# Scores of two heads on the two row halves of the array, probabilities normalised on GpSimd, and the evictions of their transposes on two engines

## The chip, the cores and the metric

The kernel runs on one core of a Trainium2 chip. The metric is the device time of one execution in microseconds (us). Beside the totals stands a profile, which is one further execution with the hardware profiler on. PE is TensorE's matmul, PEld its load of stationary operands, DVE is VectorE, ACT is ScalarE, POOL is GpSimd, and SP is the engine that issues the DMAs.

## The reference

The reference is a small network on 256 tokens of width 1024, all in fp32: a block with sparse attention (called NSA here), experts and an embedding gate; a second such block with shared keys (MOBA); and a third block with two feed-forward layers around a mixer, whose second half is a dilated attention. Three places in it are dense softmax attention on 256 keys, 64 columns a head:

```
# NSA, selected keys (and the same on window keys), 16 heads, 4 key heads
s_s = einsum('bgrqd,bgqnld->bgrqnl', qc, k_g) - slopes * dist_s
p_s = masked_softmax(s_s, dist_s >= 0)
o_s = einsum('bgrqnl,bgqnld->bgrqd', p_s, v_g)
o = gc[0] * o_c + gc[1] * o_s + gc[2] * o_w
# MOBA, 16 heads, 4 key heads
s_own = einsum('bgrqd,bgld->bgrql', qc, ko) - slopes * dist_o    # causal
pr = softmax(sc)
# mixer, 8 heads: softmax of q k with slopes, a mask and a multiplicity of each key
```

The keys are normed per head (`rms_norm(to_heads(k), k_gain)`) in NSA and MOBA and taken as they are in the mixer.

## The kernel before

**Dense products.** Every weight comes in units of 1 MB on the SP queue (`unit`, L274) into a ring of nine buffers (pool `raw`). ACT makes a unit's high part (L291), DVE what it leaves (L292), and PE multiplies three times for one product (`mm3`, L304 to L306): 48 matmuls of up to 512 columns for a column chunk of 1024 rows and 256 tokens. PE's dense products are the bulk of the program.

**What sets the order.** The program is written as one sequence, and a scheduler orders each engine's instructions ahead of time, by what each one needs and by priorities (`ahead_by`); on the chip every engine then takes its own list strictly in turn. A buffer of a pool is handed out to its users in the order in which the program asks for them; `raw` serves weight units and also `kb`, the keys of the attention.

**Keys.** In NSA, between the units of the second and the third column chunk, `keys` (L541) takes two buffers of `raw`, one for each branch (selected keys, window keys); MOBA and the mixer take one each, also between two weights. Each holds, for four key pairs, the keys of two heads on the diagonal: head 0's 64 rows beside zeros, head 1's 64 rows beside zeros in the other columns. GpSimd writes the zeros (L544), which is the buffer's first write and needs nothing but the buffer. Later `k_T` (L528) norms the keys (square L493, sum L494 and L495, reciprocal root L314 to L323, multiply L535), PE transposes them (L347), and `put_k` (L548) copies each 64-row half out of PSUM, one half on ACT (L556), one on DVE (L558). In NSA the compressed keys are made at the same time (L641 to L685): hidden products, a GELU on ACT and DVE, second products, a norm and one transpose.

**Softmax.** `softmax_T` (L561) is called for each pair of heads: 16 times in NSA (8 pairs, 2 branches), 8 in MOBA, 4 in the mixer, 28 in all. A call makes two score matmuls on all 128 rows (L565: 128 queries by 2 heads by 128 keys; L567: the other 128 queries by 2 heads by 256 keys); four fused bias, scale and maximum steps on DVE (L574); four exponentials on ACT (L579); sums and reciprocals on DVE; four multiplications of the probabilities by their weight, the first on ACT (L592), three on DVE (L594); six PE transposes (L598 to L600) into two PSUM tiles, each copied to SBUF by ACT (L601, 128x384). `attend` (L604) multiplies them with the values: four matmuls on 64 output rows each (L608, L610). Buffers: two of `p` and two of `pT`, four PSUM tiles `a` for scores and four `b` for the rest. Between the calls stand column sums for a later layer (`fill`) and, in NSA and MOBA, the second half of the queries.

The names that follow: `w` in the rows of L347 is the tile with the normed keys, `b` and `a` are PSUM tiles, `hi` and `lo` the two parts of a weight, `e` the activations.

## Time and profile before

| | |
|---|---|
| three runs | 1141.98, 1141.98, 1138.62 us |
| median | 1141.98 us |
| span of the profiled execution | 1135.9 us |
| lies around the span (median less span) | 6.1 us |
| NSA, key chain and window chunk | 42 to 59 us of the span |
| NSA, softmax of 8 pairs | 84 to 170 us |
| MOBA, key chain and query product | 361 to 385 us |
| MOBA, softmax of 8 pairs | 387 to 425 us |
| mixer, softmax of 4 pairs | 882 to 904 us |

The profiled execution's own total is not among the numbers; its span, 1135.9 us, is the time from the first to the last instruction on the core, and the 6.1 us are what the median has beyond it. A change of the span is taken as a change of the total. The stages are told from each other by the lines that run in them. A matmul's record ends later than its last column goes in, so two matmuls that follow each other overlap in their records, and the distance of their starts is their cost to PE.

### The profile page before, as it was taken

How to read it: one execution, taken by the hardware profiler on the slowest of the kernel's cores; microseconds unless marked ns; L12 is line 12 of the kernel's file. 1: busy time of each engine (PE TensorE's matmuls, PEld its weight loads, DVE VectorE, ACT ScalarE, POOL GpSimd, SP SyncE). 2: the span in 40 equal slices, each digit the busy share in tenths (PEclk: the TensorE clock that was granted, in tenths of full speed). 3: DMA queues.
4: the chain of work that ended last, by engine and by line, in shares of the span. 5: the costliest groups of instructions: out<-in, count | busy, mean ns of one | idle time of the engine just before them, and what ended most of it. 6: DMA issues, size and time to landing. Idle time of an engine off the chain costs nothing.

```text
span 1135.9 us, 18442 instructions
## 1 busy us (share of the span) xinstructions
PE 1070.6 (94%) x7133; PEld 833.2 (73%) x7133; DVE 701.9 (62%) x1672; ACT 516.2 (45%) x995; POOL 74.3 (7%) x61
## 2 busy tenths in 40 slices
PE   7999999999989999998987999999989979999995
PEld 6885548666457667665545999899879759999994
DVE  6786784644378966543467656565684775554555
ACT  5446584222267674221254444433544634444443
POOL 3000000210010002100003000000210030000001
PEclk9999999899999999999999999999989989999998
DMA  9746767599975485798886456745675344554401
GB/s 375 296 185 262 277 225 304 196 372 396 416 273 170 180 336 198 286 389 323 314 350 242 168 186 213 284 173 186 224 301 175 123 185 149 174 187 159 146 22 38
DMA packets 46508, 268.57 MB, mean 236 GB/s; under 512 B 5328, under 2 KB 7120, under 8 KB 20432
## 3 DMA queue, kind: packets, MB, share of 16 engines
q1 hardware_dynamic: 46416, 267.34, 62.9%
q8 instruction: 58, 0.95, 0.3%
q14 instruction: 34, 0.28, 0.1%
HBM read 266.27 MB, written 1.05 MB: 235 GB/s over the span
## 4 chain that ended last, share of the span: by engine, by line
PE 46%; DVE 5%; ACT 1%; issue 0%; ACTq 0%; DVEq 0%
PE b L305 8%; PE b L304 8%; PE b L306 8%; PE a L304 5%; PE a L306 5%; PE a L305 5%; PE a L1054 1%; DVE nq L319 1%; DVE h L1483 1%; PE a L1094 1%; DVE rstd L323 1%; PE a L1107 1%; PE b L1460 1%; DVE w L1482 1%; PE b L1033 0%
## 5 line engine op out<-in xcount | busy, mean ns | idle before, releaser
L292 DVE TENSOR_TENSOR lo<-raw,hi 128x1024 fp32r<-128x1024 f32 (+2 forms) x220 | 256.1, 1167 | 197.7 <-ACT hi L291 195.5
L291 ACT ACTIVATE hi<-raw 128x1024 fp32r<-128x1024 f32 (+2 forms) x234 | 234.3, 1008 | 262.3 <-PE b L305 144.6
L304 PE MATMUL b<-e,hi 128*128 128x256 f32 x768 | 219.7, 286 | 2.9 <-ACT e L426 2.9
L305 PE MATMUL b<-e,hi 128*128 128x256 f32 x768 | 219.3, 285 | 0.1
L306 PE MATMUL b<-e,lo 128*128 128x256 f32 x768 | 218.9, 285 | 0.0
L304 PE MATMUL a<-hi,e 128*128 128x512 f32 (+2 forms) x512 | 199.9, 391 | 2.4 <-ACT e L364 1.8
L305 PE MATMUL a<-lo,e 128*128 128x512 f32 (+2 forms) x512 | 198.0, 387 | 0.0
L306 PE MATMUL a<-hi,e 128*128 128x512 f32 (+2 forms) x512 | 197.2, 387 | 0.5 <-DVE e L365 0.5
L304 PEld LDWEIGHTS b<-e,hi 128*128 128x128 f32 x768 | 149.2, 194 | 4.7 <-ACT e L426 3.6
L305 PEld LDWEIGHTS b<-e,hi 128*128 128x128 f32 x768 | 149.1, 194 | 1.0 <-DVE e L427 0.7
L306 PEld LDWEIGHTS b<-e,lo 128*128 128x128 f32 x768 | 149.1, 194 | 0.0
L304 PEld LDWEIGHTS a<-hi,e 128*128 128x128 f32 x512 | 96.8, 189 | 23.1 <-ACT e L364 2.9
L306 PEld LDWEIGHTS a<-hi,e 128*128 128x128 f32 x512 | 96.1, 188 | 20.7 <-DVE e L365 2.1
L305 PEld LDWEIGHTS a<-lo,e 128*128 128x128 f32 x512 | 96.9, 189 | 18.9 <-DVE lo L292 0.9
L1054 PE MATMUL a<-raw,e 128*32 128x256 f32 x832 | 73.5, 383 | 1.1 <-DVEq L1291 0.8
L579 ACT ACTIVATE p<-p,m 128x128 f32<-128x128 f32 (+1 forms) x96 | 42.6, 447 | 8.9 <-DVE m L574 6.6
L484 DVE TENSOR_TENSOR h<-h,a 128x512 f32<-128x512 f32 x48 | 32.0, 684 | 22.0 <-PE a L1107 14.7
L1054 PEld LDWEIGHTS a<-raw,e 128*32 128x32 f32 x832 | 31.4, 109 | 18.8 <-issue 2.1
L292 POOL TENSOR_TENSOR lo<-raw,hi 128x1024 fp32r<-128x1024 f32 (+1 forms) x14 | 31.4, 2267 | 205.1 <-ACT hi L291 205.0
L1097 ACT ACTIVATE w<-a,sv 128x512 fp32r<-128x512 f32 x32 | 21.6, 687 | 48.0 <-PE a L1094 47.6
L1094 PE MATMUL a<-wd,hT 128*32 128x512 f32 x256 | 43.3, 607 | 0.0
L1107 PE MATMUL a<-w,GT 128*128 128x512 f32 x128 | 36.3, 416 | 6.2 <-ACT w L1097 5.1
(322 smaller groups left out, 1424.3 us busy)
## 6 DMA issues: line engine op xcount, KB each, us to landing
raw<-in_ffn SPq DMA_DIRECT2D x62, 1024.0 KB, 4.8
raw<-in_moe_gu SPq DMA_DIRECT2D x52, 1024.0 KB, 8.4
raw<-in_w_ada SPq DMA_DIRECT2D x36, 1024.0 KB, 5.0
wd<-in_moe_dn SPq DMA_DIRECT2D x64, 512.0 KB, 7.0
raw<-in_w_gate SPq DMA_DIRECT2D x8, 1024.0 KB, 11.1
raw<-in_w_m_in SPq DMA_DIRECT2D x8, 1024.0 KB, 5.5
raw<-in_w_a_in SPq DMA_DIRECT2D x7, 1024.0 KB, 11.1
e<-in_moe_gu SPq DMA_DIRECT2D x6, 1024.0 KB, 9.5
```

What stands on the lines that cost most here:

```text
L291: nc.scalar.activation(hi[:, sl], raw[:, at], AF.Copy)
L292: eng.tensor_tensor(lo[:, sl], raw[:, at], hi[:, sl], op=OP.subtract)
L304: mm(out, l[0], r[0], start=start, stop=False, **kw)
L305: mm(out, l[0], r[1], start=False, stop=False, **kw)
L306: mm(out, l[1], r[0], start=False, stop=stop, **kw)
L319: nc.vector.scalar_tensor_tensor(q, y, h, y, op0=OP.mult, op1=OP.mult)
L484: self.nc.vector.tensor_tensor(self.h[:, t, sl], self.h[:, t, sl], ps, op=OP.add)
L579: nc.scalar.activation(p, p, AF.Exp, bias=m[:, i:i + 1], scale=-1.0, accum_out=den[:, i:i + 1])
L1054: nc.tensor.matmul(pgs[pp][32 * x:32 * x + 32], xg[:, k, o:o + 32], wg[kk][:, x], start=(k == 0), stop=(k == KT - 1))
L1094: nc.tensor.matmul(py[32 * x:32 * x + 32], hT[:, 32 * x:32 * x + 32], wd[2 * n + x // 2][:, x % 2], start=True, stop=True)
L1097: nc.scalar.activation(yh[:, sl], py, AF.Identity, scale=cw)
L1107: nc.tensor.matmul(ps, GT[:, t * P:(t + 1) * P], y[:, n * 512:(n + 1) * 512], start=(b == 0), stop=(b == len(back) - 1))
```

## The change

The keys of all branches are one buffer of `raw` (NSA takes one buffer where it took two), four pairs by 256 keys for each branch, without zeros; no memset is left, and the first write of the buffer is now the copy of the first transposed keys. That copy takes all 128 rows at once (128x512) and alternates between ACT and DVE. A call's scores are four matmuls, two for each head, with that head's 64 rows of queries and keys as operands; a head has a PSUM tile of its own. The number of columns of a call is the same: 2 x 128 + 2 x 256. The four multiplications of the probabilities go to GpSimd. Of the two copies of the transposed probabilities the second goes to DVE. Everything else is text (docstrings).

```diff
-    sw='svvv',
+    sw='gggg',
...
-    def keys(self):
-        kb = self.raw.tile([P, 4, 2, T], F32, tag="raw", name="kb")
-        for hf in range(2):
-            self.nc.gpsimd.memset(kb[64 * hf:64 * hf + 64, :, 1 - hf], 0.0)
-        return kb
+    def keys(self, n):
+        kb = self.raw.tile([P, n, 4, T], F32, tag="raw", name="kb")
+        self.KB = [kb[:, i] for i in range(n)]
...
     def put_k(self, idx, ps, gain):
-        for hf, eng in ((0, "s"), (1, "v")):
-            sl = slice(64 * hf, 64 * hf + 64)
-            dst = self.KB[idx // 4][sl, idx % 4:idx % 4 + 2, hf, :]
...
+        dst = self.KB[idx // 4][:, idx % 4:idx % 4 + 2]
+        if gain is None:
+            self.copy(dst, ps)
+        else:
+            self.copy(dst, ps, gain)
...
-            s0 = self.psa([P, 2, P])
-            nc.tensor.matmul(s0, QT[:, j, 0:P], kb[:, :, 0:P], start=True, stop=True)
-            s1 = self.psa([P, 2, T])
-            nc.tensor.matmul(s1, QT[:, j, P:T], kb, start=True, stop=True)
+            s = [self.psa([P, 3 * P]) for _ in range(2)]
+            for t in range(2):
+                for hh in range(2):
+                    sl = slice(64 * hh, 64 * hh + 64)
+                    nc.tensor.matmul(s[hh][:, t * P:t * P + (t + 1) * P], QT[sl, j, t * P:(t + 1) * P],
+                                     kb[sl, 0:(t + 1) * P], start=True, stop=True)
...
-            for i, (p, s, a, b) in enumerate(blocks):
-                if K["sw"][i] == "s":
-                    nc.scalar.activation(p, p, AF.Copy, scale=w[:, i:i + 1])
-                else:
-                    self.engine(K["sw"][i]).tensor_scalar(p, p, w[:, i:i + 1], None, op0=OP.mult)
+            for i, (o, x, a) in enumerate(blocks):
+                self.engine(K["sw"][i]).tensor_scalar(o, o, w[:, i:i + 1], None, op0=OP.mult)
...
-                nc.scalar.activation(pT[:, hh], ps, AF.Copy)
+                if hh:
+                    nc.vector.tensor_copy(pT[:, hh], ps)
+                else:
+                    nc.scalar.activation(pT[:, hh], ps, AF.Copy)
...
-        self.KB = [self.keys() for _ in range(2)]
+        self.keys(2)
...
-        self.KB = [self.keys()]
+        self.keys(1)
```

The change also moves instructions. The lines of the changed kernel are, behind `softmax_T`, four lower than before (L641 is L637, L347 stays). Numbers ahead of a row are its place in the engine's list. First PE in NSA, from the hidden products of the compressed keys on. Before:

```order
98 L641 MATMUL b<-raw,e 64x256 x32
99 L304 MATMUL a<-hi,e 128x304
100 L305 MATMUL a<-lo,e 128x304
101 L306 MATMUL a<-hi,e 128x304
...
115 L651 MATMUL b<-consts,x_398 128x128 x2
116 L305 MATMUL a<-lo,e 128x304
117 L306 MATMUL a<-hi,e 128x304
118 L304 MATMUL a<-hi,e 128x304
119 L665 MATMUL b<-small,w_407 128x64
120 L305 MATMUL a<-lo,e 128x304
```

And now:

```order
98 L637 MATMUL b<-raw,e 64x256 x32
99 L647 MATMUL b<-consts,x_398 128x128 x2
100 L661 MATMUL b<-small,w_407 128x64
101 L665 MATMUL b<-small,w_408 128x64
102 L661 MATMUL b<-small,w_407 128x64
103 L665 MATMUL b<-small,w_408 128x64 x7
104 L678 MATMUL b<-consts,kd 128x128
105 L347 MATMUL b<-consts,w_479 128x128 x8
106 L304 MATMUL a<-hi,e 128x304 x2
107 L305 MATMUL a<-lo,e 128x304
```

The products of the third chunk (128x304) stood directly behind the hidden products, with the small matmuls of the compressed keys between them one at a time; now all of these, and the eight transposes of the first branch's keys, stand ahead of the first product.

ACT at the same place. Before:

```order
14 L291 ACTIVATE hi<-raw 128x608 x4
15 L644 ACTIVATE x_398<-b 128x256
16 L647 ACTIVATE x_398<-x_398 128x256
17 L291 ACTIVATE hi<-raw 128x512
18 L657 ACTIVATE w_407<-b 128x4x16
```

And now:

```order
14 L640 ACTIVATE x_398<-b 128x256
15 L643 ACTIVATE x_398<-x_398 128x256
16 L653 ACTIVATE w_407<-b 128x4x16 x2
17 L670 ACTIVATE w_434,kcs<-b 128x64
18 L493 ACTIVATE w_458<-w_241 128x256
19 L493 ACTIVATE w_461<-w_241 128x256
20 L667 ACTIVATE vc<-b 128x256
21 L261 ACTIVATE kb<-b,small 128x512
22 L291 ACTIVATE hi<-raw 128x608 x4
```

The four splits of that chunk (128x608) stood ahead of the whole chain of the compressed keys; now they stand behind it and behind the first copy into `kb`.

PE in MOBA, around the transposes of the keys (L347), with the last products of keys and values above in the new list and products of the queries in all other rows. Before:

```order
1023 L306 MATMUL a<-hi,e 128x512
1024 L347 MATMUL b<-consts,w_3849 128x128 x2
1025 L304 MATMUL a<-hi,e 128x512
1026 L305 MATMUL a<-lo,e 128x512
1027 L347 MATMUL b<-consts,w_3849 128x128 x6
1028 L306 MATMUL a<-hi,e 128x512
```

And now:

```order
926 L305 MATMUL a<-lo,e 128x512
927 L306 MATMUL a<-hi,e 128x512
928 L347 MATMUL b<-consts,w_3870 128x128 x8
929 L304 MATMUL a<-hi,e 128x512 x2
930 L305 MATMUL a<-lo,e 128x512
```

Before, 37 of the 96 query products stood ahead of these transposes; now none does, and on ACT and DVE no split of the query weight stands ahead of the copy into `kb`. In the mixer the values' weight stands behind the copy of the keys in the same way.

Last, PE at the end of a call of the softmax in NSA, as it is now:

```order
405 L564 MATMUL a<-kb,e 128x128 x2
406 L564 MATMUL a<-kb,e 128x256
407 L593 MATMUL b<-consts,p 128x128 x6
408 L564 MATMUL a<-kb,e 128x256
409 L604 MATMUL b<-pT,e 64x256 x2
```

The scores of one call (L564) aren't always neighbours: here the second head's 256 columns stand behind the six transposes of another call.

## Rows read from the trace of the kernel before

**Rows 1.** The page, busy time of each engine: share of the span, number of instructions.

```profile
PE 1070.6 (94%) x7133; PEld 833.2 (73%) x7133; DVE 701.9 (62%) x1672; ACT 516.2 (45%) x995; POOL 74.3 (7%) x61
```

**Rows 2.** Busy time by stretch, columns in the head row: NSA's key chain, then two softmax stages.

```profile
core 0: us, PE busy (x) PEld busy (x) DVE busy (x) ACT busy (x) POOL busy (x), PEclk, DMA share, GB/s
42.40:59.10 16.70, 16.59 (x130) 15.96 (x129) 12.89 (x51) 9.76 (x20) 0.00 (x0) 1.00 1.00 415
84.00:170.00 86.00, 82.91 (x506) 45.62 (x506) 65.49 (x312) 57.65 (x194) 0.00 (x0) 0.98 0.65 250
...
387.00:425.00 38.00, 36.33 (x209) 21.30 (x208) 27.40 (x135) 30.29 (x104) 0.00 (x0) 1.00 0.73 280
```

**Rows 3.** Timeline, NSA's key chain on PE, then DVE: start, us, engine, line, operation.

```profile
40.30 2.11 PE L641 MATMUL b<-raw,e 128*64 128x256 f32 x18
42.34 0.41 PE L304 MATMUL a<-hi,e 128*128 128x304 f32 x1
...
42.72 0.30 PE L306 MATMUL a<-hi,e 128*128 128x304 f32 x1
42.86 0.30 PE L304 MATMUL a<-hi,e 128*128 128x304 f32 x1
...
59.09 0.39 PE L304 MATMUL a<-hi,e 128*128 128x512 f32 x1
...
49.73 0.69 DVE L292 TENSOR_TENSOR lo<-raw,hi 128x512 fp32r<-128x512 f32 x1
...
56.06 1.42 DVE L535 TENSOR_TENSOR w<-w,knr 128x256 f32<-128x256 f32 x4
```

**Rows 4.** Timeline, MOBA's key chain: DVE, PE, ACT and again DVE.

```profile
361.53 0.97 DVE L263 TENSOR_SCALAR w<-a,rstd 128x256 f32<-128x256 f32 x2
...
368.76 1.22 DVE L292 TENSOR_TENSOR lo<-raw,hi 128x1024 fp32r<-128x1024 f32 x1
...
370.29 1.43 DVE L535 TENSOR_TENSOR w<-w,knr 128x256 f32<-128x256 f32 x4
...
371.92 0.82 PE L347 MATMUL b<-consts,w 128*128 128x128 f32 x6
...
374.45 1.06 ACT L291 ACTIVATE hi<-raw 128x1024 fp32r<-128x1024 f32 x1 [0.74 <-ACT kb L556]
...
374.62 0.75 DVE L263 TENSOR_SCALAR w<-a,rstd 128x512 f32<-128x512 f32 x1
```

**Rows 5.** Busy time in and behind a stall; the clock stands ahead of the DMA share.

```profile
200.00:205.00 5.00, 2.50 (x17) 2.37 (x18) 4.86 (x14) 3.35 (x7) 4.25 (x4) 0.83 0.05 20
205.00:210.00 5.00, 5.00 (x18) 4.32 (x18) 4.78 (x18) 0.51 (x1) 2.01 (x2) 0.50 0.48 154
```

**Rows 6.** Timeline of PE in calls of NSA's softmax.

```profile
86.69 0.59 PE L565 MATMUL a<-kb,e 128*128 128x256 f32 x2
87.12 1.02 PE L567 MATMUL a<-kb,e 128*128 128x512 f32 x2
88.07 2.47 PE L1447 MATMUL a<-raw,c 128*32 128x512 f32 x20
...
96.72 0.65 PE L608 MATMUL b<-pT,e 128*64 128x256 f32 x4
```

**Rows 7.** Groups by line and shape: busy us, mean ns of one, idle before, its releaser.

```profile
L601 ACT ACTIVATE pT<-b 128x384 f32<-128x384 f32 x56 | 24.5, 487 | 14.9 <-PE b L600 14.7
...
L594 DVE TENSOR_SCALAR p<-p,w 128x256 f32<-128x256 f32 x56 | 17.3, 347 | 0.0
...
L592 ACT ACTIVATE p<-p,w 128x128 f32<-128x128 f32 x28 | 11.0, 394 | 1.7 <-DVE w L588 0.9 <-DVE w L586 0.8
...
L594 DVE TENSOR_SCALAR p<-p,w 128x128 f32<-128x128 f32 x28 | 7.9, 284 | 0.5
```

**Rows 8.** Groups of POOL by line and shape, the same columns.

```profile
L1004 POOL TENSOR_TENSOR G<-G,G 128x256 fp32r<-128x256 f32 x16 | 12.2, 760 | 152.9 <-DVE G L1002 133.4 <-DVE slg L1188 12.6 <-DVE rr L1024 5.0
...
L544 POOL MEMSET kb<- 64x1024 f32 x8 | 7.6, 950 | 190.8 <-DVE lo L292 190.6
```

More of the change, by code (lines that the diff above doesn't have):

```diff
@@ L575, in softmax_T @@
+            m = self.stat([P, 4], "m")
+            p = self.pp_p.tile([P, 2, 3 * P], F32, tag="p", name="p")
+            blocks = [(p[:, hh, t * P:t * P + (t + 1) * P], s[hh][:, t * P:t * P + (t + 1) * P], (1 - t) * P)
+                      for t in range(2) for hh in range(2)]
+            for i, (o, x, a) in enumerate(blocks):
+                nc.vector.tensor_tensor_reduce(out=o, in0=x, in1=dist[:, a:2 * P], scale=-float(slopes[2 * j + i % 2]),
                                                scalar=3e38, op0=OP.add, op1=OP.min, accum_out=m[:, i:i + 1])
@@ L589, in softmax_T @@
                                         gate, op=OP.mult)
-            for i, (p, s, a, b) in enumerate(blocks):
-                if K["sw"][i] == "s":
-                    nc.scalar.activation(p, p, AF.Copy, scale=w[:, i:i + 1])
-                else:
-                    self.engine(K["sw"][i]).tensor_scalar(p, p, w[:, i:i + 1], None, op0=OP.mult)
+            for i, (o, x, a) in enumerate(blocks):
+                self.engine(K["sw"][i]).tensor_scalar(o, o, w[:, i:i + 1], None, op0=OP.mult)
             pT = self.pp_p.tile([P, 2, 3 * P], F32, tag="pT", name="pT")
@@ L597, in softmax_T @@
                 ps = self.psb([P, 3 * P])
-                nc.tensor.transpose(ps[:, 0:P], p0[:, hh], self.ident)
-                nc.tensor.transpose(ps[:, P:2 * P], p1[:, hh, 0:P], self.ident)
-                nc.tensor.transpose(ps[:, 2 * P:], p1[:, hh, P:T], self.ident)
-                nc.scalar.activation(pT[:, hh], ps, AF.Copy)
+                for k in range(3):
+                    nc.tensor.transpose(ps[:, k * P:(k + 1) * P], p[:, hh, k * P:(k + 1) * P], self.ident)
+                if hh:
+                    nc.vector.tensor_copy(pT[:, hh], ps)
+                else:
+                    nc.scalar.activation(pT[:, hh], ps, AF.Copy)
         return pT
@@ L1562, in mixer @@
         self.dense_T(x, "w_m_in", 4, put_q, per)
-        self.KB = [self.keys()]
+        self.keys(1)
         self.dense_T(x, "w_m_in", 4, lambda b, ps: self.put_k(2 * b, ps, None), 2 * per)
```

19 lines of the change are left out of this document (4 added, 15 removed).

## The prediction

> **What bounds the kernel now.** I read the busy times first: PE is busy for 94% of the span [rows 1]. So a change is worth what it does to PE's queue: work taken off, and idle time that opens. In the stretches that the change touches, PE is busy 16.59 us of 16.7 in NSA's key chain, 82.91 of 86 in NSA's softmax and 36.33 of 38 in MOBA's [rows 2]. The second view is the timeline of the key chains. What the reader is to see there is that PE doesn't wait while ACT and DVE make the keys: the hidden products end at 42.41 (40.30 + 2.11), and a product of the third weight chunk starts at 42.34 [rows 3]. In MOBA six of the keys' transposes run at 371.92, straight behind query products [rows 4]. Dense products hide both chains. The third view, the groups of the softmax, gives the prices of the steps that move.
>
> **The keys' first write (the large loss).** Before, a memset on GpSimd opens `kb`; nothing is queued behind it that matters. Now the copy of the first keys opens it, and in the new lists all that comes behind the buffer in the program, the splits and products of the next weight, stands behind that copy on ACT, DVE and PE. The products wait in PE's list behind the transposes of the keys, although their weight has long been there. The weight's load on SP also stands later, but its wait is for a buffer that is free early, so I cost it at nothing; the splits on ACT and DVE are late next.
>
> NSA: L535, the last step of the keys' norm on DVE, ends at 57.48 (56.06 + 1.42). From 42.41 that is 15.1 us, in which DVE also makes splits: four like the 0.69 us at 49.73 [rows 3] and one of 1024 columns, 1.22 as at 368.76 [rows 4]. Those 4.0 us stand behind the chain now, so L535 ends near 42.4 + 11.1 = 53.5. Then come four transposes, estimated at 0.5 since six take 0.82, a copy of 128x512 at 0.75 (as L263 at 374.62) [rows 4] and a split, about 0.7: PE's first product starts near 55.4. What it then has to do is 48 products of 304 columns, 0.14 us from start to start (42.72 to 42.86) [rows 3], and 48 of 256 columns, 0.12 by their columns: 12.4 us, to 67.8. Before, the next chunk started at 59.09 [rows 3]. **Loss 8.7 us.** Bounds: 6.5, if waits inside the chain go with the splits, and 12.7, if the chain keeps all its present length.
>
> MOBA: from L263 at 361.53 to L535's end at 371.72 are 10.2 us, with four splits of 1.22 in them [rows 4]; alone the chain takes 5.3, to 366.8. Transposes 0.5, copy 0.75 and a high part of 1.06 [rows 4] bring the first query product to 369.1, where before PE went on with one at 361.5: 7.6 us, less the eight transposes, which now lie inside the idle time (six took 0.82 [rows 4]), so 0.9 less. **Loss 6.7 us**; bounds 5 and 10.
>
> Clock: PE is idle or nearly so for 12 and 7 us there. After a stall that left PE busy for 2.50 us of 5, the granted clock was 0.83, and in the next 5 us 0.50, which is the lower of TensorE's two levels, 1.2 GHz, with PE busy all the time [rows 5]. That costs 2.5 us behind the stall. I take 2 for each chain, **4 us**; bounds 1 and 6.6.
>
> Mixer: the values' weight also stands behind the copy of the keys, but there is no norm in that chain, only products, a copy and splits. I take 1.5 us, an estimate from a copy (0.75) and a split (1.06) [rows 4] that lie one behind the other; bounds 0 and 3.
>
> **The scores.** L565 and L567 start 0.43 us apart, so 256 columns of fp32 cost PE 0.43 and a call's 768 cost 1.28 [rows 6]; 28 calls make 35.9 us. The columns stay the same, but a head uses only 64 rows, so two heads may run side by side, and a call would cost 0.64. No row of before shows two products on different rows that run side by side with one set of columns. The nearest is L608, whose two heads use different columns of the array: four records, two for each head, are through in 0.65 us [rows 6], where one after the other they would take 0.86 and the latency of a record. I take side by side, since there two products on two parts of the array do overlap. I then walked PE's new list: a product starts no earlier than the one ahead of it and not before its half is free. As the list often has something between the two heads, or one head's two products in a row, the scores come to 22.0 us, not 17.9: **13.9 us saved.** Ends: 0 (one after the other) and 17.9. Against it stand changes of shape: L567 to L1447 takes 0.95 us instead of the 0.86 that its columns need [rows 6], so 0.09, and something on the next. The scores had the shape of the transposes beside them; now they have one of their own. Some 30 changes more at 0.1: **3 us lost**; ends 0 and 5.
>
> The Trainium skill, "TensorE: Matmul & The Clock Gate", Part 3, says that matmuls on different row groups run at the same time, and gives 3.07 times for four of 32 rows. By that rule the sum is the one made here; without it the saving is 0 and the time 13.9 us longer. No row of before shows which.
>
> **Normalising on GpSimd.** Taken off: 28 x 0.394 us on ACT; 56 x 0.347 and 28 x 0.284 on DVE [rows 7]. Added: 112 multiplications on GpSimd, which has nothing else in these stretches (0.00 busy) [rows 2]. No row shows one. The nearest are the two-input operation L1004, 0.76 us for 128x256, and the memset L544, 0.95 for 1024 columns, thus 0.24 for 256 [rows 8]. I take 0.45 for 256 columns, between them, and 0.27 for 128: 1.44 for a call, ends 0.75 and 2.4. The first head's transposes need three of the four, about 1.0 us, where DVE's three took 0.98 by their records: no difference; the second head waits some 0.5 longer. That is met by the next step. No other work queues behind these on GpSimd in the softmax stages.
>
> **Evictions.** ACT copied both heads' transposes one after the other, 0.487 each [rows 7]; now DVE takes the second at the same time, so it is ready about 0.49 us earlier, minus what DVE is behind. DVE gives 0.98 and takes about 0.55 (estimated between 128x256 at half of 0.97 and 128x512 at 0.75 [rows 4]), so it isn't loaded more. Normalising and evicting together: **0**, ends -4 and +10, the latter as a rival. The memsets (8 x 0.95 us) were on an idle engine, and the keys' copies lie in the chains: 0. The buffer of `raw` that NSA no longer takes lets one more weight unit come early, but PE doesn't wait for weights in the stretches here: 0, end -2.5, which is 1 MB at 415 GB/s [rows 2].
>
> **Sum.** 8.7 + 6.7 + 4 + 1.5 = 20.9 lost in the chains, 13.9 - 3 = 10.9 won in the scores: +10.0 us on the span of 1135.9. The median stands 6.1 us above the span, which I keep: 1141.98 + 10.0 = 1152.0.
>
> **Rivals.**
> (a) The two halves of the array take turns, and the change doesn't do what it says. For it: no row shows the opposite. Against: L608 [rows 6]. The time is 13.9 longer: 1166.
> (b) GpSimd works at the pace of L1004: 2.4 us for a call instead of 0.98 beside 0.394. Less 0.49 from the eviction that is 0.9 longer; PE can hide it behind the other call in more than half of the cases. At 0.4 x 28 x 0.9 that is 10 us: 1162. Against: two inputs are read there, one here. The Trainium skill, "GPSIMD Engine Reference", 4.1 Engine selection, speaks for this one: it gives elementwise work to VectorE and calls GpSimd about 2 times slower with two inputs, at about line rate with one. Twice L594's 0.347 and 0.284 is 2.5 us for a call, which is this rival; line rate is the forecast.
> (c) Faster: the softmax runs at the pace of its chain, not of PE, and ACT is the link that gives. ACT is freed of 0.394 + 0.487 = 0.88 us in each call [rows 7], 24.7 us in all. It decides from 13.4 us on (10.0 and 0.3%), or 0.48 us of each call. With 0.6 of each call 17 us are won: 10.0 - 17 = -7, 1135. For it: in MOBA ACT is busy 30.29 us of 38. Against: PE is idle only 3.1 and 1.7 us in the two stages [rows 2], and before its copies ACT waits 14.7 us for PE [rows 7], so PE would have to be the one that was late.
> (d) All ends meet: the clock costs 1, the changes of shape 1, scores save 17.9, the rest as in the sum: 20.9 - 3 - 17.9 + 1 = +1, 1143.
>
> **How the numbers follow.** Forecast 0.50, with 1147 to 1158 as its own range; (a) 0.15, (b) 0.12, (c) 0.12, (d) 0.11. About 0.3%, 3.4 us, is what a measurement of this kernel can tell from no change. Slower: 0.77; within: 0.11; faster: 0.12. The range is 1140 to 1167: it takes in (a), (b) and (d), and leaves out (c) and a little at the top.
>
> **What would show it.** In the profile after: PE idle between the hidden products and the first product of 304 columns, about 12 us with only small matmuls in it, and 7 us in MOBA ahead of the first query product, each followed by a granted clock under 1; if these aren't there, the forecast falls. Two score records that start together, or 0.43 us apart (a). POOL's multiplication of 128x256 near 0.45 us, or 0.76 (b). The softmax stages about 8 us (NSA) and 3 us (MOBA) shorter; if they shrink by twice that, (c).

## The result and the profile after

| | before | after |
|---|---|---|
| median of the runs | 1140.3 us (4 runs) | 1256.4 us (4 runs) |
| ratio | | 1.103, interval 1.100 to 1.106 |
| span of the profiled execution | 1135.9 us | 1254.6 us |
| granted clock, mean | 0.977 | 0.918 |

The changed kernel is 116 us slower. 1152 was forecast and 1167 was the top of the range, so the sign was right and the size was missed by a factor of ten. A fourth run of the kernel before made its median 1140.3 us. The 6.1 us that were counted as lying around the span were too many: the profiled execution of the changed kernel took 1256.4 us, 1.8 more than its span.

Where the 118.7 us of span came from, by stretches between marks that both traces have (a softmax stage runs from its first score to its last attend):

| stretch | before | after | difference |
|---|---|---|---|
| start to NSA's first score | 84.0 | 98.3 | +14.3 |
| NSA's softmax | 90.2 | 139.3 | +49.1 |
| to MOBA's first score | 212.2 | 228.2 | +16.0 |
| MOBA's softmax | 39.6 | 57.8 | +18.2 |
| to the mixer's first score | 454.5 | 454.7 | +0.2 |
| mixer's softmax | 23.2 | 41.5 | +18.3 |
| to the end | 232.2 | 234.8 | +2.6 |

Of the mixer's 18.3 some 10.4 are the values' products, which stand inside the stage now and stood ahead of it before; the stretch ahead of it would be shorter by 8.6, had the second experts not taken 138.0 us instead of 129.2. Of the 16.0 ahead of MOBA's first score 10.2 lie behind the first experts, where MOBA's key chain runs; the first experts themselves took 120.5 us instead of 117.8.

Busy time in NSA's key chain and in the three softmax stages of the changed kernel, and last NSA's softmax in the kernel before. The head row names the columns; [rows 2] answers to the first three:

```profile
core 0: us, PE busy (x) PEld busy (x) DVE busy (x) ACT busy (x) POOL busy (x), PEclk, DMA share, GB/s
43.00:60.00 17.00, 10.25 (x50) 7.56 (x47) 10.31 (x46) 5.49 (x14) 0.00 (x0) 0.69 0.56 237
98.30:237.60 139.30, 118.60 (x604) 63.23 (x603) 63.76 (x282) 50.88 (x169) 51.65 (x64) 0.71 0.46 172
465.80:523.60 57.80, 47.97 (x250) 26.81 (x251) 30.49 (x124) 29.12 (x92) 27.67 (x32) 0.82 0.53 205
978.30:1019.80 41.50, 37.36 (x165) 24.61 (x164) 24.58 (x92) 17.61 (x33) 13.12 (x16) 0.84 0.37 127
...
84.00:174.20 90.20, 87.11 (x536) 48.51 (x535) 66.71 (x313) 61.12 (x201) 0.00 (x0) 0.98 0.67 258
```

The reader is to see two things. PE is idle for 20.7 of 139.3 us in NSA's softmax, where it was idle for 3.1 of 90.2. And while it is busy it is slower: the clock is 0.71 there, against 0.98. No engine is full: GpSimd, which has the new work, is busy for 37% of the stage. So this doesn't look like an engine that became the bound, but like a chain; the experiments below test that.

The groups of POOL in the changed kernel (busy us, mean ns of one, idle before and its releasers), to be held beside [rows 8]:

```profile
L588 POOL TENSOR_SCALAR p<-p,w 128x256 f32<-128x256 f32 x56 | 53.3, 964 | 0.0
L588 POOL TENSOR_SCALAR p<-p,w 128x128 f32<-128x128 f32 x56 | 39.9, 724 | 319.6 <-DVE w L585 107.2 <-DVE w L583 89.0 <-ACT p L576 84.9
...
L1000 POOL TENSOR_TENSOR G<-G,G 128x256 fp32r<-128x256 f32 x16 | 11.7, 730 | 165.8 <-DVE G L998 140.8 <-DVE slg L1184 16.8 <-DVE rr L1020 6.1
```

A multiplication by a scalar of 128x256 takes 0.96 us, longer than the operation with two inputs on the same shape (0.73). Four of them are 3.4 us a call. What that does is seen in the timeline of one call in MOBA (POOL, then PE):

```profile
482.48 3.77 POOL L588 TENSOR_SCALAR p<-p,w 128x128 f32<-128x128 f32 x4 [4.34 <-PE a L1443]
...
483.92 0.33 PE L593 MATMUL b<-consts,p 128*128 128x128 f32 x1 [0.64 <-POOL p L588]
485.40 0.55 PE L593 MATMUL b<-consts,p 128*128 128x128 f32 x3 [1.15 <-POOL p L588]
486.30 0.54 PE L593 MATMUL b<-consts,p 128*128 128x128 f32 x2 [0.35 <-POOL p L588]
```

PE does a transpose, waits for the next multiplication, does three, waits again.

The key chain of NSA on PE, beside [rows 3]:

```profile
37.71 6.64 PE L637 MATMUL b<-raw,e 128*64 128x256 f32 x60
47.10 0.44 PE L647 MATMUL b<-consts,x 128*128 128x128 f32 x2 [2.74 <-DVE x L644]
...
49.54 3.23 PE L665 MATMUL b<-small,w 128*128 128x64 f32 x14 [0.19 <-DVE w L656]
...
55.55 2.12 PE L347 MATMUL b<-consts,w 128*128 128x128 f32 x8 [2.29 <-DVE w L535]
58.41 0.88 PE L304 MATMUL a<-hi,e 128*128 128x304 f32 x2 [0.74 <-ACT hi L291]
```

The hidden products end at 44.35 and the first product of the third chunk starts at 58.41, where it was 42.41 and 42.34. The 14 small products (L669 before, L665 now) take 3.23 us; the granted clock was 0.51 from 49.5 to 52.8 us, its lower level, and 0.69 in the mean of 43 to 60. In MOBA the same is seen, PE waiting for the keys and then for a split of the query weight:

```profile
436.02 2.12 PE L347 MATMUL b<-consts,w 128*128 128x128 f32 x8 [5.01 <-DVE w L535]
439.86 0.79 PE L304 MATMUL a<-hi,e 128*128 128x512 f32 x1 [1.72 <-ACT hi L291]
```

The scores do run side by side. In MOBA's first two calls all eight records of a call lie in 0.93 us, the latency of the last one included, where 768 columns one after the other need 1.28 [rows 6]:

```profile
465.82 0.93 PE L564 MATMUL a<-kb,e 64*128 64x128 f32 x8
466.98 0.93 PE L564 MATMUL a<-kb,e 64*128 64x128 f32 x8 [0.24 <-ACT e L523]
```

In the records behind these rows the two heads' first products start 6 ns apart (465.816 and 465.822). But this isn't the rule: a product leaves two records, 224 in all, so 112 could start beside one of the other head, and only 56 start within 20 ns of another.

### The profile page after: what moved, and what is told of

Its sections match the earlier page's. It is cut to its first block, busy times and chain, and to the rows that moved or that the text cites. A ratio compares the mean times of both kernels' runs of the same rounds, so it can differ in the third digit from the quotient of the medians.

```text
span 1254.6 us, 18640 instructions
## 1 busy us (share of the span) xinstructions
PE 1138.7 (91%) x7245; PEld 865.5 (69%) x7245; DVE 694.8 (55%) x1612; ACT 496.2 (40%) x935; POOL 158.2 (13%) x165
## 4 chain that ended last, share of the span: by engine, by line
PE 42%; DVE 5%; ACT 1%; POOL 1%; issue 1%; POOLq 0%; ACTq 0%; DVEq 0%
PE b L305 7%; PE b L304 7%; PE b L306 7%; PE a L304 5%; PE a L306 5%; PE a L305 5%; PE a L1050 1%; DVE nq L319 1%; DVE h L1479 1%; PE a L1090 1%; POOL p L588 1%; DVE rstd L323 1%; PE a L1103 1%; PE b L1456 1%; DVE w L1478 0%
## 5 line engine op out<-in xcount | busy, mean ns | idle before, releaser
L292 DVE TENSOR_TENSOR lo<-raw,hi 128x1024 fp32r<-128x1024 f32 (+2 forms) x220 | 255.7, 1167 | 200.5 <-ACT hi L291 198.1
L304 PE MATMUL a<-hi,e 128*128 128x512 f32 (+2 forms) x512 | 204.2, 400 | 5.0 <-ACT hi L291 2.5
L305 PE MATMUL a<-lo,e 128*128 128x512 f32 (+2 forms) x512 | 202.3, 395 | 0.0
L306 PE MATMUL a<-hi,e 128*128 128x512 f32 (+2 forms) x512 | 199.8, 393 | 0.3 <-DVE e L365 0.2
L588 POOL TENSOR_SCALAR p<-p,w 128x128 f32<-128x128 f32 (+1 forms) x112 | 92.4, 844 | 319.6 <-DVE w L585 107.2
L304 PEld LDWEIGHTS a<-hi,e 128*128 128x128 f32 x512 | 99.1, 194 | 27.7 <-ACT hi L291 3.8
L305 PEld LDWEIGHTS a<-lo,e 128*128 128x128 f32 x512 | 99.5, 194 | 20.7 <-DVE lo L292 2.3
L306 PEld LDWEIGHTS a<-hi,e 128*128 128x128 f32 x512 | 98.7, 194 | 21.7 <-DVE e L365 1.9
L1050 PE MATMUL a<-raw,e 128*32 128x256 f32 x832 | 78.1, 398 | 5.8 <-PEq L1309 5.8
L593 PE MATMUL b<-consts,p 128*128 128x128 f32 x168 | 44.8, 374 | 26.0 <-POOL p L588 25.6
L593 PEld LDWEIGHTS b<-consts,p 128*128 128x128 f32 x168 | 23.7, 177 | 52.6 <-POOL p L588 49.9
L595 DVE COPY pT<-b 128x384 f32<-128x384 f32 x28 | 15.6, 558 | 64.5 <-PE b L593 64.5
L576 ACT ACTIVATE p<-p,m 128x128 f32<-128x128 f32 (+1 forms) x96 | 42.5, 446 | 18.0 <-DVE m L571 17.7
```

The source lines that it names most:

```text
L292: eng.tensor_tensor(lo[:, sl], raw[:, at], hi[:, sl], op=OP.subtract)
L304: mm(out, l[0], r[0], start=start, stop=False, **kw)
L305: mm(out, l[0], r[1], start=False, stop=False, **kw)
L306: mm(out, l[1], r[0], start=False, stop=stop, **kw)
L576: nc.scalar.activation(o, o, AF.Exp, bias=m[:, i:i + 1], scale=-1.0, accum_out=den[:, i:i + 1])
L588: self.engine(K["sw"][i]).tensor_scalar(o, o, w[:, i:i + 1], None, op0=OP.mult)
```

## The experiments

Ratios are to the kernel before on the same chip. Two theories stood at the start. **A**: GpSimd's pace is the main cause, the key chains the second, and the rest of the change is harmless or better. **B**: the softmax is long by the scores' new shape or the eviction on DVE.

### First: GpSimd alone

```diff
 # the kernel before
-    sw='svvv',
+    sw='gggg',
```

> The kernel before, with only the four multiplications of the probabilities moved to GpSimd; keys, scores and evictions as before. Theory A (GpSimd's pace is the main cause: in the changed kernel one multiplication took 0.60 us for 128x128 and 0.92 for 128x256, 3.06 us a call, with PE waiting for it): 28 calls x 3.06 less what one call hides of another, 60 to 95 us, so 1200 to 1235 us. Rival B (the loss in the softmax comes from the other parts, that is from the scores' new shape or the copy of the transposes on DVE): under 20 us more than before, at most 1160.

1182.0 us, ratio 1.038 (1.036 to 1.041): +42. NSA's softmax took 112.5 us (90.2 before), MOBA's 51.7 (39.6), the mixer's 24.9 (23.2). The clock in NSA's stage was 0.91. The time lies between the two expectations: GpSimd's work alone costs 42 us, a third of the loss, where 60 to 95 were expected. (Its 3.06 us a call were made of the smallest and the median record; the means give 3.38.)

### Second: all but GpSimd

```diff
 # the changed kernel
-    sw='gggg',
+    sw='svvv',
...
+                if K["sw"][i] == "s":
+                    nc.scalar.activation(o, o, AF.Copy, scale=w[:, i:i + 1])
+                else:
```

> The changed kernel with the multiplications back on ACT (first) and DVE (three); keys, scores and evictions as changed. Theory A: the softmax stages lose their 86 us and win about 8 by the scores, the two key chains stay: 1140 + 31 - 8, so 1155 to 1172 us. Rival B: the softmax stays long, over 1200.

1208.4 us, ratio 1.060 (1.057 to 1.062): 48 less than with GpSimd, but above A's range and inside B's (over 1200). NSA's softmax was still at 114.9 us, so a part of the loss there isn't GpSimd's.

### Third: the early first write

```diff
 # the changed kernel
     def keys(self, n):
         kb = self.raw.tile([P, n, 4, T], F32, tag="raw", name="kb")
+        self.nc.gpsimd.memset(kb[:, :, 0, 0:1], 0.0)
```

> The changed kernel with one small memset by GpSimd (one column of each key pair's first keys) as the first write of the keys' buffer, which puts the next weight's splits and products ahead of the key chains again; multiplications stay on GpSimd. Theory A with the chains as the second cause: the 31 us that the stretches ahead of the softmax had lost in NSA and MOBA come back, less 0 to 8: 1217 to 1236 us. Rival C (PE's idle time in the chains is made up elsewhere, or the stretches are long for another reason): 1245 to 1256.

1211.3 us, ratio 1.065 (1.061 to 1.070): 45 less than the changed kernel, more than expected. PE's list has the products of the third chunk directly behind the hidden products again, and the trace shows it:

```profile
39.95 2.98 PE L638 MATMUL b<-raw,e 128*64 128x256 f32 x26
42.85 0.41 PE L304 MATMUL a<-hi,e 128*128 128x304 f32 x1
```

Stretch by stretch against the changed kernel: start to NSA's first score -13.6, NSA's softmax -5.5, to MOBA's first score -11.1, MOBA's softmax -3.5, and from MOBA's softmax to the end of the mixer's -13.4. Of the last, 10.1 lie in the second experts, from the product that gathers the first tokens to the last one that adds up (127.9 us instead of 138.0). Their first products had begun with a wait of 3 us and a clock of 0.58 from 549 to 560 us in the changed kernel. So the chains cost what they hold up (24.7 us) and as much again behind them.

### Fourth: both undone

```diff
 # the third kernel with the multiplications of the second
-    sw='gggg',
+    sw='svvv',
```

> The changed kernel with both: the multiplications back on ACT and DVE, and the small memset as first write. What is left of the change is the scores by row halves, the one full copy of the keys and the second eviction on DVE. Theory A: nothing is left that costs, the scores bring 8 to 14 us: 1126 to 1136. Rival B: slower than before, over 1145. If the gain of the scores is lost to changes of the array's shape: 1137 to 1143.

1171.6 us, ratio 1.028 (1.026 to 1.030). With both known causes gone, 32 us are left, so A isn't enough. NSA's softmax took 113.2 us at a clock of 0.83, PE idle for 13.1 of them:

```profile
85.00:198.20 113.20, 100.08 (x608) 59.23 (x609) 75.26 (x331) 56.41 (x186) 0.00 (x0) 0.83 0.57 212
```

In one place the clock falls while PE has no wait that the rows mark (line, shape, count):

```profile
119.64 0.48 PE L565 MATMUL a<-kb,e 64*128 64x128 f32 x2
120.06 0.66 PE L697 MATMUL a<-kc,e 128*128 128x64 f32 x4
...
121.65 0.70 PE L565 MATMUL a<-kb,e 64*128 64x256 f32 x2
122.28 0.90 PE L697 MATMUL a<-kc,e 128*128 128x64 f32 x4
123.11 2.50 PE L565 MATMUL a<-kb,e 64*128 64x256 f32 x10
127.00 1.08 PE L1447 MATMUL a<-raw,c 128*32 128x512 f32 x4 [1.39 <-DVE m L572]
```

Four small products (L697) take 0.66 us twice and then 0.90. From 122 to 130 us the clock was 0.53, and from 116 to 122, with PE busy but for waits of under 0.2 us and scores of 64 rows among small products, 1.00. That gave two theories for the rest, both about the scores. **D1**: PE's new list, which puts up to 16 scores in a row (15 in NSA) and then has nothing to cover the chain. **D2**: products of 64 rows let the clock fall. **F** is B's other half, the eviction and the keys' copies.

### Fifth: scores by row halves alone

```diff
 # the kernel before
-            s0 = self.psa([P, 2, P])
-            nc.tensor.matmul(s0, QT[:, j, 0:P], kb[:, :, 0:P], start=True, stop=True)
-            s1 = self.psa([P, 2, T])
-            nc.tensor.matmul(s1, QT[:, j, P:T], kb, start=True, stop=True)
+            s = [self.psa([P, 3 * P]) for _ in range(2)]
+            for t in range(2):
+                for hh in range(2):
+                    sl = slice(64 * hh, 64 * hh + 64)
+                    nc.tensor.matmul(s[hh][:, t * P:t * P + (t + 1) * P], QT[sl, j, t * P:(t + 1) * P],
+                                     kb[sl, hh, 0:(t + 1) * P], start=True, stop=True)
```

> The kernel before, with only the scores made by row halves: four products of 64 rows, a PSUM tile for each head, read from the keys' two diagonal parts. Memset, keys' copies, multiplications and evictions as before. Theory D (the 64-row scores are what is left: about 32 us): 1160 to 1176. Rival F (what is left comes from the eviction on DVE or the keys' full copies): at most 1140, faster than before.

1162.6 us, ratio 1.021 (1.020 to 1.023): +24. The part that was to win 11 us loses 24.

### Sixth: the eviction alone

```diff
 # the kernel before
-                nc.scalar.activation(pT[:, hh], ps, AF.Copy)
+                if hh:
+                    nc.vector.tensor_copy(pT[:, hh], ps)
+                else:
+                    nc.scalar.activation(pT[:, hh], ps, AF.Copy)
```

> The kernel before, with only the second eviction of the transposed probabilities moved from ACT to DVE. Theory D: within 6 us of before, 1134 to 1146. Rival F: over 1155.

1149.3 us, ratio 1.010 (1.008 to 1.011): +10.5, between the two expectations, and a loss. In NSA's softmax (101.0 us) DVE now waits in its list for PE's transposes, with the next call's bias and maximum steps behind it:

```profile
DVE pT L602 <- PE b L600: 8.5, 9, 2.8
```

(us in all, times, longest.) Before, DVE had no operation in that place. The total hides a part of the cost: the three softmax stages took 16.9 us more than before, and the first experts 7.2 less (110.6 instead of 117.8). In these stages the fifth kernel lost 15.8 and the fourth 30.7, so there the two add up; in the totals, 24 + 10.5 against 32, they nearly do. The one full copy of the keys, which the fourth kernel also has, was run in no kernel by itself; these sums leave little or nothing for it.

### Seventh: scores two calls ahead, no more

```diff
 # the fourth kernel
+            seen = self.turned.setdefault(id(QT), [])
+            with self.tc.issue_after(seen[-2].ins) if len(seen) >= 2 else nullcontext():
                 for t in range(2):
...
-                    nc.tensor.transpose(ps[:, k * P:(k + 1) * P], p[:, hh, k * P:(k + 1) * P], self.ident)
+                    last = nc.tensor.transpose(ps[:, k * P:(k + 1) * P], p[:, hh, k * P:(k + 1) * P], self.ident)
...
+            seen.append(last)
         return pT
```

> The fourth kernel (multiplications on ACT and DVE, early first write of the keys' buffer) with one rule more for PE's list: the scores of a call stand behind the last transpose of the call two before. Its list then reads one or two scores between transposes and attend, where without the rule up to 15 scores stand in a row. Theory D1 (the list is the cause: scores of several calls in a row, then nothing on PE to cover the chain of ACT and DVE, and the clock falls in the waits): most of the 32 us come back, 1135 to 1152. Rival D2 (products of 64 rows by themselves let the clock fall): 1160 or more.

1210.2 us, ratio 1.062 (1.055 to 1.068): 39 slower than the fourth. NSA's softmax took 132.7 us at a clock of 0.73. So scores in a row aren't the harm; that they keep the chains of several calls going is what this suggests, and isn't shown. D1 in this form falls. That the time is above 1160 doesn't show D2, since the list was changed too.

### Eighth: one more full product in each call

```diff
 # the fourth kernel
             s = [self.psa([P, 3 * P]) for _ in range(2)]
+            nc.tensor.matmul(s[0][:, 0:T], QT[:, j, 0:P], kb, start=True, stop=True)
```

> The fourth kernel with one more product on all 128 rows by 256 columns in each call, ahead of its scores and into the same PSUM tile, whose values the scores then overwrite: 0.43 us each at full clock, 12 us in all. Rival D2: the clock stays up, faster than the 1172 of the fourth kernel, 1150 to 1165. Theory D1: PE only gets more work, part of it in its waits: 1172 to 1184.

1163.3 us, ratio 1.023 (1.020 to 1.025): 8 less than the fourth with more work. The clock in NSA's softmax was 0.94 instead of 0.83, but that stage got only 2.5 us shorter, and MOBA's 2.0. The larger part, 10.3 us, lies in the first experts, 110.4 instead of 120.7 us: a wait of PE for its own sequencer at a branch (5.0 us in the fourth kernel) is gone. So the clock was higher where PE got more full products, and the total says little about it.

### Ninth: the same list, full rows

```diff
 # the fifth kernel
-                    nc.tensor.matmul(s[hh][:, t * P:t * P + (t + 1) * P], QT[sl, j, t * P:(t + 1) * P],
-                                     kb[sl, hh, 0:(t + 1) * P], start=True, stop=True)
+                    nc.tensor.matmul(s[hh][:, t * P:t * P + (t + 1) * P], QT[:, j, t * P:(t + 1) * P],
+                                     kb[:, hh, 0:(t + 1) * P], start=True, stop=True)
```

> The fifth kernel (before, with scores by four products and a PSUM tile for each head), but each product on all 128 rows, against the keys' block of the head with its zeros: the list of PE is the same instruction by instruction, only the 64 rows become 128, and no two heads run side by side (17.9 us more of columns than if all did). Theory D2 (the 64-row shape is the cause, by the clock): the clock stays up and the time lies below the fifth kernel's 1162, at 1140 to 1155. Rival D1 (the new list is the cause, whatever the shape): 1162 to 1180.

1156.4 us, ratio 1.014 (1.012 to 1.016), between the two. This is the cleanest comparison of the study, since PE's list is the same as the fifth's instruction by instruction. NSA's and MOBA's softmax, first in the fifth kernel (64 rows), then in this one (128 rows):

```profile
84.70:189.70 105.00, 94.46 (x611) 55.57 (x611) 67.31 (x314) 61.80 (x201) 0.00 (x0) 0.89 0.60 228
408.80:450.20 41.40, 37.92 (x251) 23.35 (x251) 28.59 (x137) 31.49 (x105) 0.00 (x0) 0.96 0.65 255
```

```profile
84.10:186.20 102.10, 93.63 (x611) 59.20 (x612) 67.28 (x314) 62.24 (x201) 0.00 (x0) 0.93 0.61 235
404.70:444.80 40.10, 38.34 (x251) 26.07 (x251) 28.58 (x137) 31.06 (x105) 0.00 (x0) 1.00 0.67 264
```

With up to 17.9 us more of columns the full products are 6 us faster in all; the clock is 0.93 and 1.00 instead of 0.89 and 0.96. So the row halves win nothing here. The traces show where the columns went. On PE, from each score's start to the next instruction's and without waits, the scores of all calls took 38.9 us before, 42.2 in the ninth kernel and 34.6 in the fifth: 7.6 us fewer by the row halves, not 17.9, for 59 of 112 records start within 20 ns of another. In NSA's and MOBA's softmax, where 6.5 of the 7.6 lie, the clock that wasn't granted is 6.8 us more in the fifth (13.6 instead of 6.8) and PE's idle time 3.7 more (14.0 instead of 10.3). And 17 us of the fifth's 24 stay with full rows: these belong to what comes with four products and a PSUM tile for each head. By stretches 11.9 us lie in NSA's softmax (102.1 instead of 90.2; PE idle for 8.5 us instead of 3.1, clock 0.93 instead of 0.98) and 4.3 in the first experts.

### Tenth: a factor in the instruction

```diff
 # the third kernel
-                self.engine(K["sw"][i]).tensor_scalar(o, o, w[:, i:i + 1], None, op0=OP.mult)
+                self.engine(K["sw"][i]).tensor_scalar(o, o, 0.0078125, None, op0=OP.mult)
```

> The third kernel (changed, early first write, multiplications on GpSimd), but GpSimd multiplies by a constant in the instruction and not by each row's weight; so the normalisation and the gate of the probabilities are left out, and nothing waits for the reciprocals. If the price of 0.60 and 0.92 us lies in reading the factor of each partition: 0.3 and 0.5 us, and 1175 to 1195. If it lies in GpSimd's pace over the elements: the same 0.6 and 0.9, and 1200 to 1212.

The total (1222.9 us) can't be read, because this kernel leaves the normalisation out and the experts are chosen from other values then: the second experts took 158.9 us instead of 127.9. The price can:

```profile
L589 POOL TENSOR_SCALAR p<-p 128x256 f32<-128x256 f32 x56 | 48.4, 877 | 12.0 <-ACT p L577 11.9
L589 POOL TENSOR_SCALAR p<-p 128x128 f32<-128x128 f32 x56 | 30.6, 557 | 261.4 <-ACT p L577 197.4 <-DVE den L580 64.1
```

0.88 and 0.56 us in place of 0.95 and 0.69 in the third kernel. A factor per partition is the smaller part of the price; the larger stays with a constant, and 128 more columns cost 0.32 us there.

### Eleventh: two wide products

```diff
 # the first kernel
-            for i, (p, s, a, b) in enumerate(blocks):
-                if K["sw"][i] == "s":
-                    nc.scalar.activation(p, p, AF.Copy, scale=w[:, i:i + 1])
-                else:
-                    self.engine(K["sw"][i]).tensor_scalar(p, p, w[:, i:i + 1], None, op0=OP.mult)
+            for i, (q, n) in enumerate(((p0, P), (p1, T))):
+                nc.gpsimd.tensor_tensor(q, q, w[:, 2 * i:2 * i + 2, None].to_broadcast([P, 2, n]), op=OP.mult)
```

> The first kernel (before, multiplications on GpSimd), with two products of two tensors for each call in place of four by a scalar: 128x256 and 128x512 with the weights spread over the columns. By the rows of before these take 0.76 and 1.28, 2.04 us a call in place of 3.06. Theory A (PE waits for GpSimd's time in the chain): 42 us over before become 20 to 32, 1160 to 1172. Rival (it is the presence of GpSimd, not its time): 1178 to 1190.

1148.4 us, ratio 1.007 (1.006 to 1.009): +9 instead of +42, better than expected. The same arithmetic on the same engine, with two tensors:

```profile
L591 POOL TENSOR_TENSOR p<-p,w 128x512 f32<-128x512 f32 x28 | 30.1, 1073 | 0.0
...
L591 POOL TENSOR_TENSOR p<-p,w 128x256 f32<-128x256 f32 x28 | 19.6, 700 | 266.3 <-DVE w L588 109.6 <-ACT p L579 79.3 <-DVE w L586 71.6
```

1.77 us a call, where the four scalar ones took 3.33 in the first kernel (2 x 0.98 + 2 x 0.68). 28 x 1.56 is 44 us; 34 were won.

### Twelfth: one of four on GpSimd

```diff
 # the kernel before
-    sw='svvv',
+    sw='gvvv',
```

> The kernel before, with only the first of the four multiplications (128x128) on GpSimd instead of ACT: 0.60 us in place of 0.394, beside DVE's three of about 0.8 in all. Theory A: it ends with DVE's, no wait is added, 1134 to 1146. Rival (DVE and GpSimd get in each other's way): 1150 or more, with longer records of L594 or of the GpSimd operation.

1139.1 us, ratio 1.000 (0.999 to 1.001). One operation beside DVE's three leaves the total where it was, as A says. That it is free isn't shown: the three softmax stages took 3.2 us more than before and the stretch behind NSA's 4.3 more, and the first experts 8.3 less (109.5 instead of 117.8). Its record was 0.73 us, and DVE's 128x256 took 0.379 us instead of 0.347 [rows 7], so DVE was a little slower beside it:

```profile
L594 POOL TENSOR_SCALAR p<-p,w 128x128 f32<-128x128 f32 x28 | 20.4, 727 | 292.3 <-DVE w L588 109.6 <-DVE w L586 95.1 <-ACT p L579 79.9
L594 DVE TENSOR_SCALAR p<-p,w 128x256 f32<-128x256 f32 x56 | 19.2, 379 | 0.0
```

### Thirteenth: the change with two wide products

```diff
 # the changed kernel
-            for i, (o, x, a) in enumerate(blocks):
-                self.engine(K["sw"][i]).tensor_scalar(o, o, w[:, i:i + 1], None, op0=OP.mult)
+            for t in range(2):
+                o = p[:, :, t * P:t * P + (t + 1) * P]
+                nc.gpsimd.tensor_tensor(o, o, w[:, 2 * t:2 * t + 2, None].to_broadcast([P, 2, (t + 1) * P]), op=OP.mult)
```

> The changed kernel with GpSimd's four multiplications by a scalar replaced by two products of two tensors (128x256 and 128x512, 0.70 and 1.07 us in the eleventh kernel, 1.77 us a call instead of 3.3). If the form of GpSimd's operation makes the part of the loss that moving it back to ACT and DVE won (48 us), most of that is won here: 1212 to 1230. If in this kernel the chain is long for other reasons: 1240 or more.

1225.5 us, ratio 1.074 (1.071 to 1.078), as expected: 31 of the 48 us that GpSimd costs inside the change are the form of its operation. The operations took 1.11 and 0.76 us there.

### Fourteenth: the code moved

```diff
 # the ninth kernel, in nsa, behind gained_T
+        extra = self.psb([P, 18])
+        for i in range(18):
+            nc.tensor.matmul(extra[:, i:i + 1], self.ident, self.ident[:, i:i + 1], start=True, stop=True)
```

> The ninth kernel with 18 small products of one column put early into PE's list (2 us of PE), whose values nobody reads; the list behind them is the same. In the ninth kernel PE waits 4.8 us for its own sequencer at the branch of the first experts' overflow, and the clock falls behind it. If that wait hangs on how many instructions stand ahead of the branch (1297 and near it in every kernel that has it, 1265 to 1274 and 1314 in those that don't): the wait is 0.3 us and the time 4 to 10 us shorter, 1147 to 1153. If it belongs to the new list: no shorter, 1156 to 1160.

1155.7 us, ratio 1.014 (1.012 to 1.016): no shorter in all, but for a reason of its own, and the wait did hang on the place. The wait is gone (this kernel, then the ninth: us in all, times, longest),

```profile
PE a L1058 <- PEq L1317: 0.3, 1, 0.3
```

```profile
PE a L1055 <- PEq L1314: 5.1, 2, 4.8
```

and the first experts took 113.4 instead of 122.1 us. The 18 small products, put at 2 us, cost 7.6: the third chunk started at 50.1 instead of 42.5. So where the instructions come to lie costs the ninth kernel 8.7 us in the first experts. That isn't what it loses there against the kernel before, which has no such wait. The first experts, before, in the ninth and in the fourteenth kernel:

```profile
204.20:322.00 117.80, 112.58 (x931) 66.17 (x932) 52.20 (x145) 28.80 (x67) 7.93 (x9) 0.96 0.92 362
```

```profile
218.30:340.40 122.10, 113.00 (x919) 64.08 (x917) 48.03 (x137) 28.20 (x66) 5.26 (x8) 0.93 0.89 347
```

```profile
223.90:337.30 113.40, 108.17 (x919) 63.11 (x917) 48.95 (x137) 28.23 (x66) 6.11 (x8) 0.98 0.95 371
```

Before, the granted clock was 0.50 from 203.3 to 210.1 and from 309.1 to 312.5 us of the span; in the ninth kernel it was 0.50 from 214.1 to 220.9 and, behind the wait, from 285.8 to 299.5. The sixth, eighth and twelfth kernels, with the clock at 1.00 there, took 109.5 to 110.7 us. So against the kernel before, the fourth, fifth, seventh and ninth lose 2.9 to 5.4 us in the first experts and the changed kernel 2.7, and totals that differ by under 8 us have to be read by stages.

### Fifteenth: GpSimd beside DVE

```diff
 # the kernel before
-            for i, (p, s, a, b) in enumerate(blocks):
-                if K["sw"][i] == "s":
...
+            nc.gpsimd.tensor_tensor(p0, p0, w[:, 0:2, None].to_broadcast([P, 2, P]), op=OP.mult)
+            for i, (p, s, a, b) in list(enumerate(blocks))[2:]:
+                nc.vector.tensor_scalar(p, p, w[:, i:i + 1], None, op0=OP.mult)
```

> The kernel before with the first 128 queries' two multiplications as one product of two tensors on GpSimd (128x256, 0.70 us) and the other two on DVE (2 x 0.35), so that ACT and DVE each have one operation less and GpSimd ends with DVE. If the softmax has room at ACT and DVE: 1128 to 1136, faster than both. If PE's work and the list bound it: 1137 to 1142. If a first operand of the transposes comes later: 1143 to 1150.

1144.0 us, ratio 1.004 (1.003 to 1.005), the third case of the expectation. Beside GpSimd's product DVE's multiplications took 0.473 us instead of 0.347 [rows 7], and PE waited for the first transpose's operand (4.4 us in all):

```profile
L592 DVE TENSOR_SCALAR p<-p,w 128x256 f32<-128x256 f32 x56 | 24.6, 473 | 0.3
L590 POOL TENSOR_TENSOR p<-p,w 128x256 f32<-128x256 f32 x28 | 19.8, 707 | 295.3 <-DVE w L588 99.9 <-ACT p L579 86.0 <-DVE w L586 82.8
...
L596 PE MATMUL b<-consts,p 128*128 128x128 f32 x56 | 15.3, 305 | 4.4 <-POOL p L590 4.4
```

No division of the multiplications that was tried beats the kernel before, and no other kernel here does.

## Why the prediction was wrong

**The sum, step by step.** What each part costs, by undoing it in the changed kernel or doing it alone:

| step | forecast | alone, on before | undone, in the change |
|---|---|---|---|
| keys' first write, with clock and mixer | +20.9 | | -45 |
| scores by row halves | -10.9 | +24 | |
| normalising on GpSimd | 0 | +42 | -48 |
| second eviction on DVE | 0 | +10.5 | |

45 + 24 + 48 + 10.5 is 127, against a measured 116. The parts were taken in two frames and share waits, so the sum is a check of size and no proof.

**Keys' first write: mechanism right, size missed by half.** The idle stretch, the late chunk and the fallen clock are where they were put. The first product of 304 columns came at 58.4 instead of 55.4, since the hidden products ended 2 us later and the eight transposes ran at the low clock (2.12 us); MOBA's first query product came at 439.86, behind transposes that had waited 5 us for L535. The term for the chains was 15.4 + 4 and they held the softmax up by 24.7. What had no term is what follows: 9 us in NSA's and MOBA's softmax, about 10 in the second experts, and the mixer, where the values' products lie inside the softmax. The experiment shows that these come back with the early write; by which waits in between wasn't traced.

**Scores: the step "side by side, so 13.9 us are saved" failed.** Products of two heads do run side by side, as chosen against rival (a), and as the Trainium skill's page "TensorE: Matmul & The Clock Gate", Part 3, says of row groups; the 6 ns between the heads agree with it. Two things failed. The walk through the list put the scores at 22.0 us; they took 34.6 in the fifth kernel, 4.3 less than the 38.9 before by the same count, since about half of the records found no partner. And saved columns were taken for saved time. By the ninth kernel, four products and a tile for each head give another list, which costs 17 us even with full rows: 11.9 in span in NSA's softmax, in more idle time and at a lower clock, and 4.3 in the first experts. With 64 rows the clock is lower still, by as much as the scores got shorter (6.8 us not granted against 6.5). What in the list lengthens NSA's chains stays open.

**GpSimd: the price failed, and so did its upper end.** This is the step that cost most. The multiplication was taken at 0.45 and 0.27 us, with L1004's 0.76 for two inputs as the top for 256 columns. It took 0.96 and 0.72. The assumption behind the bound, that one input can't be dearer than two, was wrong on this engine, and the eleventh kernel beside the first shows it for the same work: 0.70 us for 128x256 with two tensors, 0.98 with one and a scalar. The Trainium skill, "GPSIMD Engine Reference", 4.1 Engine selection, gives one input at about line rate and two at about half of VectorE's speed. The rows here have it the other way around, and the measurement decides. Its advice to leave elementwise work to VectorE was right, by a factor of 2.8 here (0.964 to 0.347 us [rows 7]). Rival (b) named the mechanism and the chain and priced it at 10 us, since it counted 0.4 of 28 calls and 0.9 us in each. In the first kernel a call's four took 3.33 us beside the 0.98 of DVE's three, 2.35 more or 66 us in all, and 42 were lost: 0.6 of it. In NSA's softmax PE was idle for 15.5 us and the clock 0.91, where it was 3.1 and 0.98:

```profile
85.10:197.60 112.50, 96.99 (x543) 50.52 (x541) 56.66 (x266) 57.93 (x185) 51.36 (x64) 0.91 0.55 209
```

**Eviction: taken as relief for ACT, it was a wait for DVE.** The sum compared busy times, and the price was right: 0.55 us was estimated and the copy took 0.558. But DVE takes its list in turn, so the copy's wait for PE's transposes (8.5 us in the sixth kernel) stands ahead of the next call's steps.

**What the prediction's base missed.** PE at 94% was read as "PE's work is the bound". In the softmax stages PE's list interleaves chains that fit closely, and work taken off PE there didn't shorten them (the fifth kernel against the ninth). In NSA's softmax every experiment had more idle time on PE than the 3.1 us before, and none a clock above 0.98; but the clock doesn't follow the idle time alone, for the sixth kernel had 9.1 us of it at 0.97 and the ninth 8.5 at 0.93. The clock not granted is 0.082 of 1254.6 us, 103 us, against 0.023 of 1135.9, 26 us: 77 more, 56 of them in the three softmax stages, and part of it in waits, where it costs nothing. The forecast had 4 us for it.

Of the rivals, (a) is refuted by the trace, (c) by the experiments that took work off ACT (the sixth and the fifteenth slower, the twelfth the same), (d) by the result.

## What to carry to other kernels

Ask of a removed instruction what else it did: a memset was the buffer's first write, and with it gone the ring handed the next weights out behind a long chain. A price for an operation that no row shows needs a wider top than the dearest neighbour, above all on another engine, and a form with more inputs may be the cheaper one. Where a stage is a web of chains close to full, price a change by the longest chain and by the clock that its waits cost, and not by the busy time that it takes off.

## What was not expected of the hardware

- GpSimd multiplies 128x256 fp32 by a scalar per partition in 0.95 to 0.98 us, by a constant in 0.88, and by a second tensor spread over the columns in 0.70 to 0.76. In the fifteenth kernel DVE's multiplication of 128x256 beside the last form took 0.473 us instead of 0.347.
- Products of 64 rows, two heads side by side, left the granted clock lower than the same list with 128 rows: 0.89 against 0.93 in NSA's softmax, 0.96 against 1.00 in MOBA's. In the fourth kernel the clock went to its lower level at 122.5 us, though PE had had no wait over 0.2 us since 116.
- At the branch of the first experts PE waited 4.8 to 6.1 us for its own sequencer in the nine kernels (the changed one among them) whose program for PE has 1293 to 1305 instructions up to there, and 0.3 to 0.4 us in the eight with 1267 to 1274, 1315 and 1316. Moving the code by 18 instructions took it away. What lies behind it wasn't looked at. The first experts took from 109.5 to 123.2 us in sixteen of the kernels with the same work, by this wait and by where the clock was low.
